# A gated three-branch decoder layer on one core: first loads issued in order of use, a third load buffer, and gate tiles between attention and branch projection

## The chip, the cores and the metric

The kernel runs on one core of a Trainium2 chip. The metric is device time in microseconds (us) of one execution. The core has TensorE (PE in the profile; PEld is its loading of weights), VectorE (DVE), ScalarE (ACT), GpSimd (POOL) and SyncE (SP). In this kernel SP issues every DMA, one after the other.

## What is computed

One decoder layer on 256 tokens of width 2048, in float32:

```python
proj = x @ w_in
q_a, k_a, v_a, z_a, u_g, v_g, z_g, q_c, z_c, g_logit = jnp.split(proj, split_at, axis=-1)
y_a = _moba_attention(q_a, k_a, v_a) * jax.nn.silu(z_a)      # 8 heads, causal
y_g = _spatial_gating(u_g, v_g, w_s, b_s, ln_v_g, ln_v_b) * jax.nn.silu(z_g)
mem_k = (mem @ w_mem_k); mem_v = (mem @ w_mem_v)             # 256 memory tokens
y_c = _memory_attention(q_c, mem_k, mem_v) * jax.nn.silu(z_c)  # 4 heads
gates = jax.nn.sigmoid(g_logit)
merged = (gates[:, :, 0] * (y_a @ w_branch_attn)
          + gates[:, :, 1] * (y_g @ w_branch_sgu)
          + gates[:, :, 2] * (y_c @ w_branch_mem))
y = merged @ w_out
x = _layer_norm(DN_ALPHA * x + y, ln_g, ln_b)
```

The spatial gating applies GELU to u and v, a layer norm to v, and a causal 128x128 mixing matrix for each of 8 channel groups.

## The kernel before

**Precision.** Every float32 operand of a large product is taken apart by split() (lines 57 to 60): ScalarE copies it to a rounded `hi` (line 59), VectorE subtracts to get `lo` (line 60), and PE adds up three products, hi x hi, hi x lo and lo x hi. In the profile `hi` and `lo` are the weights of the classic stream, `sh` and `sl` those of the S stream.

**Start.** mem_values() (8 chunks of `w_mv`) and then mem_keys() (8 chunks of `w_mk`) project the memory tokens. Beside mem_keys the list `x_work` (from x_stages()) prepares x: its hi and lo parts (`xhl`), four sums of its quadrants (`F`) and their parts (`xw`), which are stored to DRAM (`xf`) for later. x comes in two loads of 1 MB (`X`), called in mem_values at kp 5 and 6. After mem_keys six blocks of `w_st` are loaded (s_load) and two S steps prepared (s_prep).

**Two streams.** After that a loop at the end of the function runs two generators in steps. classic() makes the gate tiles (gate_tiles: zc, za, ug), the memory attention, the block attention, the spatial gating and the three branch projections (gated_branch). s_stream() makes the eight 1024-wide projections whose results are taken with tokens on partitions (three pairs of branch gates, v_a and v_g), each unit as seven products M1, M5, M6, M3, M7, M4, M2 of quadrants, two steps each, 112 steps in all. In M5, M6 and M4 VectorE subtracts blocks before the split, in M3 after it (line 289). One S step is 12 matmuls of 512 columns; one classic step is half a tile (8 k-slices, each a matmul of 512 and one of 256 columns) or a quarter of a branch's column block (12 matmuls of 512). The loop takes an S step while

```python
done_s * (C_STEPS - LEAD - TAIL) < (done_c - LEAD) * S_STEPS    # 160, 2, 14; 112
```

so that the S stream ends with classic step 146, whatever that step holds. s_prep prepares two S steps ahead; c_half prepares two halves ahead.

**Small work.** Evacuations go into `late` and are emitted behind the next step's matmuls. Attention heads and the gating's mixing go as lists of stages into `pending`; each tick() emits the next stage of each list. A tile's end calls tick(), gated() calls it too. drain() yields an empty classic step, and further ones with a tick() each until `pending` is empty; classic() runs it before each of the three branch projections, since a branch reads the y of all heads. It takes 4, 4 and 2 steps.

**Loads.** The weights of the classic stream come in chunks of 1 MB, two halves each, in the order of the list `chunks`, into tag `raw` with two buffers. prep_half() splits a half; once both halves of chunk i are split it loads chunk i + 2. Loads and stores of all kinds share SP's queue, and the order of instructions on each engine is made by a planner from the program order, its own estimate of times and the buffers that are free; a load for which a buffer is free can be issued long before its place in the program. `vg` (tag vg, 1 MB) holds the v of the gating, from unit 5 of the S stream to the last mixing.

**End.** merged() transposes the merged branches, 16 chunks of `w_o` give the output projection, and residual() and normalise() finish.

Of the kernel before, what the change touches and what calls it, by code (L numbers as in the profile page):

```python
# [14 lines left out]
P = 128  # L15
# [12 lines left out]
def decoder_layer(ctx, tc, xT, memT, x_tok, w_st, w_mv, w_mk, w_zc, w_qc, w_za, w_qk, w_ug, w_zg,  # L28
# [60 lines left out]

    def load_chunk(i):  # L90
        t = wts.tile([P, 2, 1024], F32, tag="raw", name=f"raw{i}", bufs=2)
        raw[i] = t
        if i < 8:
            a = w2(f"mraw{i}", (P, 2, S))
            act_raw[i] = a
            if i == 0:

                for kk in range(2):
                    nc.sync.dma_start(a[:, kk], memT[:, kk])
                    for c in (slice(0, 512), slice(512, 1024)):  # L100
                        nc.sync.dma_start(t[:, kk, c], chunks[i][:, kk, c])
                return
            nc.sync.dma_start(a, memT[:, 2 * i:2 * i + 2, :])
        for h in range(2) if i < 4 else (slice(0, 2),):
            nc.sync.dma_start(t[:, h], chunks[i][:, h])

    def prep_half():
        i, h = divmod(ptr["half"], 2)
        while ptr["load"] <= min(i + 1, len(chunks) - 1):
            load_chunk(ptr["load"])  # L110
            ptr["load"] += 1
        ptr["half"] += 1
        if i in held_at:
            hi, lo = held_at[i](h)
            split(hi, lo, raw[i][:, h].rearrange("p (k c) -> p k c", c=S))
        else:
            hi = wts.tile([P, 1024], F32R, tag="hi", name=f"hi{i}_{h}", bufs=3)
            lo = wts.tile([P, 1024], F32R, tag="lo", name=f"lo{i}_{h}", bufs=3)
            n = 512 if i == 0 else 1024
            for c in range(0, 1024, n):  # L120
                split(hi[:, c:c + n], lo[:, c:c + n], raw[i][:, h, c:c + n])
            ready.append((hi, lo))
        if h == 1:
            del raw[i]
            if ptr["load"] < len(chunks) and ptr["load"] <= i + 2:
                load_chunk(ptr["load"])
                ptr["load"] += 1
# [6 lines left out]
    for w in (w_mv, w_mk, w_zc, w_qc):  # L134
        chunks += [w[j] for j in range(8)]
    chunks += [w_br[2 * 8 + j] for j in range(8)]
    chunks += [w_za[j] for j in range(8)]
    chunks += [w_qk[j] for j in range(16)]
    chunks += [w_br[j] for j in range(8)]
    chunks += [w_ug[j] for j in range(8)]  # L140
# [13 lines left out]

    for j in range(16):
        if j >= 12:
            pass
# [225 lines left out]
    def mem_values():  # L383
        ps = [[new_acc(f"mv{t}{n}") if t + n < 2 else new_sps(f"mv{t}{n}") for n in range(2)] for t in range(2)]
        for kp in range(8):
            if kp == 0:
                load_chunk(0)
                ptr["load"] = 1
# [6 lines left out]
            for kk in range(2):  # L395
# [9 lines left out]
                if kp in (5, 6) and kk == 0:  # L405
                    x_loads[kp - 5]()
# [30 lines left out]

    for _ in run(mem_values()):
        pass
    for i, _ in enumerate(run(mem_keys())):  # L440
        if i >= 1 and x_work:
            x_work.pop(0)()
    while x_work:
        x_work.pop(0)()
        step(lambda: None)
    for blk in (B11, B12, B22):
        for h in range(2):
            s_load(0, blk, h)
# [12 lines left out]
    def gate_tiles(w, func, d):  # L461

        for j in range(8):
# [209 lines left out]
    def gated_branch(b, order):  # L673
        for n in range(4):
# [6 lines left out]
            for half in range(4):  # L681
# [9 lines left out]
                if half == 3:  # L691
                    late.append(lambda n=n, ps=ps, g=g: gated(b, order, n, ps, g))
                yield
# [39 lines left out]
    def classic():  # L733
# [3 lines left out]
        yield from drain()  # L737
        yield from gated_branch(2, 0)
        yield from gate_tiles("za", AF.Silu, sza_d)
        new_y(0)  # L740
        yield from block_attention()
        yield from drain()
        yield from gated_branch(0, 1)
        yield from gate_tiles("ug", AF.Gelu_apprx_tanh, gu_d)
        new_y(1)
        yield from gating()
        yield from drain()
        yield from gated_branch(1, 2)

    def drain():  # L750

        yield None
        while pending:
            tick()
            yield None
# [142 lines left out]
```

## Time and profile before

| | |
|---|---|
| median of 3 runs | 1037.3 us (1035.51 to 1040.58) |
| profiled execution | 1036.3 us |
| its span, first to last instruction | 1034.6 us |
| mean granted clock of PE | 0.982 |
| busy PE / VectorE / ScalarE | 95% / 80% / 56% of the span |
| DMA | 269.28 MB, mean 260 GB/s |

A busy PE in the profile is not a PE at its peak, since matmuls are pipelined and their ends are modelled; what counts here is where PE has gaps, and where its granted clock is below 1.00. Times in the rows are microseconds from the span's start. A row of a stretch gives for each engine its busy time and the number of its instructions.

### The profile page before, as it was taken

The page shows a single profiled execution, that of the slowest core. Times are in us where ns is not written, and L with a number is a line of the kernel's source. Part 1 is how long each engine was busy: PE and PEld are TensorE (multiplying, and loading weights), DVE is VectorE, ACT ScalarE, POOL GpSimd, SP SyncE. Part 2 cuts the span into 40 slices and gives each one's busy share as a digit, 9 for nine tenths or more (in the row PEclk, how much of TensorE's full clock was granted, in tenths as well). Part 3 has the DMA queues.
Part 4 walks back from the last instruction along what each step waited for, and adds up shares of the span by engine and source line. Part 5 has one row for each costly group of instructions (what it writes and reads, how often), then busy time and mean ns, then how long its engine had stood idle before and what let it go on. Part 6 is the DMA issues. An engine that isn't in the chain of part 4 may idle for free.

```text
span 1034.6 us, 12910 instructions
## 1 busy us (share of the span) xinstructions
PE 987.9 (95%) x4888; PEld 827.9 (80%) x4888; DVE 823.0 (80%) x800; ACT 580.4 (56%) x638; POOL 7.8 (1%) x17
## 2 busy tenths in 40 slices
PE   8699999999998999999999999879989999999995
PEld 6578888888876788888888887658878888888885
DVE  6644897797788889777977998989898685775657
ACT  6433665656556565565655557766546465754440
POOL 0000000000000000000000000000000001000000
PEclk9899999999999999999999999979999999999998
DMA  9997468847945985797389558639958955678642
GB/s 339 416 403 236 170 207 327 359 146 276 337 178 197 371 340 185 264 346 300 132 300 366 175 165 322 238 122 366 413 174 315 309 174 195 222 268 294 225 158 81
DMA packets 68125, 269.28 MB, mean 260 GB/s; under 512 B 7520, under 2 KB 21600, under 8 KB 45536
## 3 DMA queue, kind: packets, MB, share of 16 engines
q1 hardware_dynamic: 68064, 268.47, 70.9%
q8 instruction: 38, 0.62, 0.2%
q14 instruction: 23, 0.19, 0.1%
HBM read 245.37 MB, written 23.07 MB: 259 GB/s over the span
## 4 chain that ended last, share of the span: by engine, by line
PE 74%; DMA 11%; DVE 8%; ACT 3%; issue 3%; SPq 0%; DVEq 0%; ACTq 0%
PE sM L365 7%; PE sM L364 7%; PE sM L366 7%; DMA raw<-in_w_mv_dram 4%; DVE sl L60 3%; PE mk L165 3%; PE q L165 3%; PE za L165 3%; PE zc L165 3%; PE qc L165 3%; PE k L165 3%; PE zg L165 3%; PE o L782 3%; PE o L781 3%; PE o L780 3%
## 5 line engine op out<-in xcount | busy, mean ns | idle before, releaser
L59 ACT ACTIVATE hi<-raw 128x1024 fp32r<-128x1024 f32 (+1 forms) x218 | 227.8, 1050 | 213.4 <-DMA raw<-in_w_o_dram 22.2
L60 DVE TENSOR_TENSOR lo<-raw,hi 128x1024 fp32r<-128x1024 f32 (+1 forms) x218 | 261.8, 1210 | 98.7 <-ACT hi L59 97.7
L60 DVE TENSOR_TENSOR sl<-b,sh 128x2048 fp32r<-128x2048 f32 x112 | 255.9, 2287 | 56.5 <-ACT sh L59 55.8
L59 ACT ACTIVATE sh<-b 128x2048 fp32r<-128x2048 f32 x112 | 214.5, 1915 | 123.2 <-PE sM L365 101.8
L289 DVE TENSOR_TENSOR b<-b,b 128x2048 f32<-128x2048 f32 x64 | 145.8, 2283 | 6.2 <-DMA b<-in_w_st_dram 6.0
L365 PE MATMUL sM<-sl,xf 128*128 128x512 f32 x256 | 103.6, 405 | 5.7 <-DVE sl L60 5.7
L364 PE MATMUL sM<-sh,xf 128*128 128x512 f32 x256 | 102.8, 402 | 1.1 <-ACT sh L59 1.1
L366 PE MATMUL sM<-sh,xf 128*128 128x512 f32 x256 | 102.6, 401 | 0.0
L365 PE MATMUL sM<-sl,xhl 128*128 128x512 f32 x192 | 75.7, 394 | 2.4 <-DVE sl L60 2.4
L364 PE MATMUL sM<-sh,xhl 128*128 128x512 f32 x192 | 76.0, 396 | 0.0
L689 PE MATMUL b<-lo,yhl 128*128 128x512 f32 x192 | 75.0, 391 | 0.5 <-DVE lo L60 0.5
L366 PE MATMUL sM<-sh,xhl 128*128 128x512 f32 x192 | 75.1, 391 | 0.0
L690 PE MATMUL b<-hi,yhl 128*128 128x512 f32 x192 | 74.0, 391 | 1.0 <-DVE yhl L60 1.0
L688 PE MATMUL b<-hi,yhl 128*128 128x512 f32 x192 | 71.7, 391 | 1.6 <-ACT hi L59 1.6
L365 PEld LDWEIGHTS sM<-sl,xf 128*128 128x128 f32 x256 | 49.5, 193 | 17.6 <-DVE sl L60 7.9
L364 PEld LDWEIGHTS sM<-sh,xf 128*128 128x128 f32 x256 | 49.3, 193 | 12.5 <-ACT sh L59 1.7
L366 PEld LDWEIGHTS sM<-sh,xf 128*128 128x128 f32 x256 | 49.5, 193 | 10.6
L165 PE MATMUL ug<-xhl,hi 128*128 128x512 f32 x128 | 45.7, 398 | 3.2 <-ACT hi L59 3.2
L402 PE MATMUL mv<-hi,memhl 128*128 128x512 f32 x128 | 37.9, 407 | 11.1 <-ACT hi L59 11.0
L165 PE MATMUL mk<-memhl,hi 128*128 128x512 f32 x128 | 46.2, 405 | 1.4 <-ACT hi L59 1.4
L165 PE MATMUL q<-xhl,hi 128*128 128x512 f32 x128 | 46.7, 401 | 0.0
L165 PE MATMUL qc<-xhl,hi 128*128 128x512 f32 x128 | 46.2, 400 | 0.0
(296 smaller groups left out, 1845.2 us busy)
## 6 DMA issues: line engine op xcount, KB each, us to landing
b<-in_w_st_dram SPq DMA_DIRECT2D x64, 1024.0 KB, 7.7
xf<-xf SPq DMA_DIRECT2D x64, 512.0 KB, 5.6
raw<-in_w_br_dram SPq DMA_DIRECT2D x24, 1024.0 KB, 6.9
raw<-in_w_qk_dram SPq DMA_DIRECT2D x16, 1024.0 KB, 7.2
raw<-in_w_o_dram SPq DMA_DIRECT2D x16, 1024.0 KB, 4.8
raw<-in_w_mk_dram SPq DMA_DIRECT2D x8, 1024.0 KB, 5.3
raw<-in_w_zc_dram SPq DMA_DIRECT2D x8, 1024.0 KB, 4.9
raw<-in_w_qc_dram SPq DMA_DIRECT2D x8, 1024.0 KB, 7.8
```

Source lines behind the costliest of these rows:

```text
L59: nc.scalar.activation(hi, v, AF.Copy)
L60: nc.vector.tensor_tensor(lo, v, hi.bitcast(F32), op=ALU.subtract)
L165: nc.tensor.matmul(ps, hi, x, start=first, stop=False)
L289: sub = lambda o, x, y: nc.vector.tensor_tensor(o, x, y, op=ALU.subtract)
L364: nc.tensor.matmul(ps, ah, hi[:, c], start=first, stop=False, skip_group_check=True)
L365: nc.tensor.matmul(ps, ah, lo[:, c], start=False, stop=False, skip_group_check=True)
L366: nc.tensor.matmul(ps, al, hi[:, c], start=False, stop=last, skip_group_check=True)
L402: nc.tensor.matmul(ps[t][n], lhs, rhs[:, n * 512:(n + 1) * 512], start=(k == 0 and rhs is hi and lhs is xh[t]), stop=(k == KT - 1 and lhs ...
L688: nc.tensor.matmul(ps[t], yh, hi[:, c], start=(k == 0), stop=False)
L689: nc.tensor.matmul(ps[t], yh, lo[:, c], start=False, stop=False)
L690: nc.tensor.matmul(ps[t], yl, hi[:, c], start=False, stop=(k == 7))
L780: nc.tensor.matmul(ps[:, 0:n], mh, hi, start=first, stop=False)
```

## The change

It does the following.

- Each of the chunks 1 to 15 is issued on SP behind the chunk before it (`issue_after` orders instructions of one queue, it does not wait for data). The two loads of X are issued behind chunks 5 and 6. The six `w_st` blocks are asked for within mem_keys, at its steps 2, 4, 10 and 12, each behind the newest chunk load; `x_work` begins one step earlier.
- Every third of the chunks 0 to 15, and every third of the 16 chunks of `w_o`, goes into the buffer of `vg`; there a load runs up to three chunks ahead instead of two. Between chunk 16 and `w_o` there are two buffers as before.
- drain() goes. Three of the eight za tiles run between memory attention and its branch projection, three of the eight ug tiles between block attention and its projection; the other five follow the projection. The list of chunks follows. Before the third projection, behind the gating, nothing takes drain's place. In the first column block of each projection the steps 0 to 2 call tick().

```diff
@@ -87,8 +87,25 @@
     ptr = {"load": 0, "half": 0}
     hold = {}
 
+    loaded = {}
+    riders = {}
+
     def load_chunk(i):
-        t = wts.tile([P, 2, 1024], F32, tag="raw", name=f"raw{i}", bufs=2)
+
+        if 0 < i < 16:
+            with tc.issue_after(loaded[i - 1].ins):
+                load_one(i)
+        else:
+            load_one(i)
+        for fn in riders.pop(i, ()):
+            with tc.issue_after(loaded[i].ins):
+                fn()
+
+    def load_one(i):
+        if i % 3 == 2 and i < 16 or i >= OUT and (i - OUT) % 3 == 2:
+            t = big.tile([P, 2, 1024], F32, tag="vg", name=f"raw{i}")
+        else:
+            t = wts.tile([P, 2, 1024], F32, tag="raw", name=f"raw{i}", bufs=2)
         raw[i] = t
         if i < 8:
             a = w2(f"mraw{i}", (P, 2, S))
@@ -98,17 +115,23 @@
                 for kk in range(2):
                     nc.sync.dma_start(a[:, kk], memT[:, kk])
                     for c in (slice(0, 512), slice(512, 1024)):
-                        nc.sync.dma_start(t[:, kk, c], chunks[i][:, kk, c])
+                        loaded[i] = nc.sync.dma_start(t[:, kk, c], chunks[i][:, kk, c])
                 return
             nc.sync.dma_start(a, memT[:, 2 * i:2 * i + 2, :])
         for h in range(2) if i < 4 else (slice(0, 2),):
-            nc.sync.dma_start(t[:, h], chunks[i][:, h])
+            loaded[i] = nc.sync.dma_start(t[:, h], chunks[i][:, h])
+
+    def room_after(i):
+
+        return i - 3 if i <= 16 or i >= OUT + 2 else i - 2
+
+    def load_after(c):
+        while ptr["load"] < len(chunks) and room_after(ptr["load"]) <= c:
+            ptr["load"] += 1
+            load_chunk(ptr["load"] - 1)
 
     def prep_half():
         i, h = divmod(ptr["half"], 2)
-        while ptr["load"] <= min(i + 1, len(chunks) - 1):
-            load_chunk(ptr["load"])
-            ptr["load"] += 1
         ptr["half"] += 1
         if i in held_at:
             hi, lo = held_at[i](h)
@@ -122,9 +145,7 @@
             ready.append((hi, lo))
         if h == 1:
             del raw[i]
-            if ptr["load"] < len(chunks) and ptr["load"] <= i + 2:
-                load_chunk(ptr["load"])
-                ptr["load"] += 1
+            load_after(i)
 
     def c_half(ahead=2):
         while len(ready) < ahead + 1 and ptr["half"] < 2 * len(chunks):
@@ -133,11 +154,13 @@
 
     for w in (w_mv, w_mk, w_zc, w_qc):
         chunks += [w[j] for j in range(8)]
+    chunks += [w_za[j] for j in range(3)]
     chunks += [w_br[2 * 8 + j] for j in range(8)]
-    chunks += [w_za[j] for j in range(8)]
+    chunks += [w_za[j] for j in range(3, 8)]
     chunks += [w_qk[j] for j in range(16)]
+    chunks += [w_ug[j] for j in range(3)]
     chunks += [w_br[j] for j in range(8)]
-    chunks += [w_ug[j] for j in range(8)]
+    chunks += [w_ug[j] for j in range(3, 8)]
     chunks += [w_zg[j] for j in range(8)]
     chunks += [w_br[8 + j] for j in range(8)]
 
@@ -152,9 +175,8 @@
             return t[:, :, 0:S], t[:, :, S:2 * S]
         return dst
 
+    OUT = len(chunks)
     for j in range(16):
-        if j >= 12:
-            pass
         chunks.append(w_o[j])
         if j in (4, 7, 10, 13):
             held_at[len(chunks) - 1] = held(*divmod((4, 7, 10, 13).index(j), 2))
@@ -384,8 +406,7 @@
         ps = [[new_acc(f"mv{t}{n}") if t + n < 2 else new_sps(f"mv{t}{n}") for n in range(2)] for t in range(2)]
         for kp in range(8):
             if kp == 0:
-                load_chunk(0)
-                ptr["load"] = 1
+                load_after(-1)
             a = act_raw.pop(kp)
             n = 1 if kp == 0 else 2
             for c in range(0, 2, n):
@@ -402,8 +423,6 @@
                             nc.tensor.matmul(ps[t][n], lhs, rhs[:, n * 512:(n + 1) * 512],
                                              start=(k == 0 and rhs is hi and lhs is xh[t]),
                                              stop=(k == KT - 1 and lhs is xl[t]))
-                if kp in (5, 6) and kk == 0:
-                    x_loads[kp - 5]()
                 yield
 
         def evacuate():
@@ -435,17 +454,22 @@
             step(go)
             yield
 
+    riders[5], riders[6] = [x_loads[0]], [x_loads[1]]
     for _ in run(mem_values()):
         pass
     for i, _ in enumerate(run(mem_keys())):
-        if i >= 1 and x_work:
+        if x_work:
             x_work.pop(0)()
+        if i in (2, 4):
+            with tc.issue_after(loaded[ptr["load"] - 1].ins):
+                s_load(0, B12, i // 2 - 1)
+        if i in (10, 12):
+            for blk in (B11, B22):
+                with tc.issue_after(loaded[ptr["load"] - 1].ins):
+                    s_load(0, blk, i // 2 - 5)
     while x_work:
         x_work.pop(0)()
         step(lambda: None)
-    for blk in (B11, B12, B22):
-        for h in range(2):
-            s_load(0, blk, h)
     s_prep(0)
     s_prep(1)
 
@@ -458,9 +482,9 @@
     def put_y(b, j, y):
         split(yhl[b][:, j, 0:S], yhl[b][:, j, S:2 * S], y)
 
-    def gate_tiles(w, func, d):
-
-        for j in range(8):
+    def gate_tiles(w, func, d, tiles=range(8)):
+
+        for j in tiles:
             def fin(ps, j=j):
                 v = w1(f"{w}{j}")
                 joined(v, ps, f"{w}{j}")
@@ -690,6 +714,8 @@
                         nc.tensor.matmul(ps[t], yl, hi[:, c], start=False, stop=(k == 7))
                 if half == 3:
                     late.append(lambda n=n, ps=ps, g=g: gated(b, order, n, ps, g))
+                elif n == 0:
+                    late.append(tick)
                 yield
 
     def gated(b, order, n, ps, g):
@@ -734,25 +760,17 @@
         yield from gate_tiles("zc", AF.Silu, szc_d)
         new_y(2)
         yield from mem_attention()
-        yield from drain()
+        yield from gate_tiles("za", AF.Silu, sza_d, range(3))
         yield from gated_branch(2, 0)
-        yield from gate_tiles("za", AF.Silu, sza_d)
+        yield from gate_tiles("za", AF.Silu, sza_d, range(3, 8))
         new_y(0)
         yield from block_attention()
-        yield from drain()
+        yield from gate_tiles("ug", AF.Gelu_apprx_tanh, gu_d, range(3))
         yield from gated_branch(0, 1)
-        yield from gate_tiles("ug", AF.Gelu_apprx_tanh, gu_d)
+        yield from gate_tiles("ug", AF.Gelu_apprx_tanh, gu_d, range(3, 8))
         new_y(1)
         yield from gating()
-        yield from drain()
         yield from gated_branch(1, 2)
-
-    def drain():
-
-        yield None
-        while pending:
-            tick()
-            yield None
 
     C_STEPS, S_STEPS = 160, 14 * UNITS
     LEAD, TAIL = 2, 14
```

## Rows read from the trace of the kernel before

**Rows 1.** The page's busy time, share of the span and instructions by engine

```profile
PE 987.9 (95%) x4888; PEld 827.9 (80%) x4888; DVE 823.0 (80%) x800; ACT 580.4 (56%) x638; POOL 7.8 (1%) x17
```

**Rows 2.** Stretches: length; busy PE, PEld, DVE, ACT, POOL; clock; DMA share; GB/s

```profile
20.00:80.00 60.00, 47.64 (x204) 37.46 (x204) 36.32 (x41) 26.74 (x32) 0.00 (x0) 0.91 0.99 402
110.00:862.00 752.00, 731.20 (x3585) 611.58 (x3584) 644.85 (x560) 447.87 (x478) 3.62 (x4) 0.99 0.71 260
```

**Rows 3.** The same view: the three stalled windows in the middle

```profile
300.00:350.00 50.00, 43.48 (x186) 33.58 (x185) 44.64 (x36) 30.30 (x34) 0.00 (x0) 1.00 0.54 193
640.00:700.00 60.00, 48.93 (x193) 37.92 (x192) 53.84 (x59) 41.83 (x48) 0.00 (x0) 0.89 0.55 206
760.00:780.00 20.00, 16.79 (x80) 13.89 (x79) 19.57 (x21) 9.75 (x10) 0.00 (x0) 0.91 0.61 189
```

**Rows 4.** The same view: three stretches without a PE gap

```profile
580.00:610.00 30.00, 30.00 (x160) 25.54 (x159) 30.00 (x27) 16.80 (x22) 0.00 (x0) 1.00 0.41 138
700.00:750.00 50.00, 50.00 (x222) 41.30 (x221) 46.58 (x38) 29.70 (x24) 0.00 (x0) 1.00 1.01 392
900.00:1020.00 120.00, 120.00 (x624) 102.73 (x623) 78.41 (x102) 51.02 (x56) 0.00 (x0) 1.00 0.61 215
```

**Rows 5.** PE's instructions in time: start, length, what, [idle before <-releaser]

```profile
6.36 0.97 PE L402 MATMUL mv<-hi,memhl 128*128 128x512 f32 x3 [0.89 <-ACT hi L59]
...
31.89 2.07 PE L402 MATMUL mv<-hi,memhl 128*128 128x512 f32 x4 [8.01 <-ACT hi L59]
```

**Rows 6.** The SP queue in time, 0 to 35 us: start, length, line, issues

```profile
12.60 1.29 SPq L230 DMA_DIRECT2D X<-in_xT_dram  x2
13.94 1.06 SPq L273 DMA_DIRECT2D b<-in_w_st_dram  x2
15.34 5.28 SPq L105 DMA_DIRECT2D raw<-in_w_mv_dram  x3
```

**Rows 7.** PE's instructions of tile sM (the S stream) by stretch

```profile
630.00:700.00 70.00, 44.28 (x161) 0.90 0.57 213
```

**Rows 8.** PE's instructions of tile b (the branch projections) by stretch

```profile
630.00:700.00 70.00, 12.27 (x48) 0.90 0.57 213
```

**Rows 9.** The chain of 60 to 76 us in time: start, length, what

```profile
64.28 0.28 PE mk L165
64.56 0.12 PE mk L166
64.68 0.23 PE mk L165
```

**Rows 10.** VectorE by line and shape, 110 to 862 us: xcount | busy, mean ns

```profile
L60 DVE TENSOR_TENSOR sl<-b,sh 128x2048 fp32r<-128x2048 f32 x112 | 255.9, 2287 | 56.5 <-ACT sh L59 55.8
L60 DVE TENSOR_TENSOR lo<-raw,hi 128x1024 fp32r<-128x1024 f32 x138 | 166.7, 1218 | 27.5 <-ACT hi L59 27.0 <-PE q L166 0.3
L289 DVE TENSOR_TENSOR b<-b,b 128x2048 f32<-128x2048 f32 x64 | 145.8, 2283 | 6.2 <-DMA b<-in_w_st_dram 6.0
L324 DVE TENSOR_TENSOR k<-sM,k 128x512 f32<-128x512 f32 x31 | 21.2, 684 | 1.9 <-PE sM L366 1.8
L700 DVE TENSOR_TENSOR sg<-b,sg 128x512 f32<-128x512 f32 x16 | 10.6, 682 | 0.0
L639 DVE TENSOR_TENSOR vg<-vg,sc 128x256 f32<-128x256 f32 x16 | 6.2, 420 | 1.8 <-DMA sc<-in_sgu_bc_dram 1.8
...
L612 DVE BATCH_NORM_STATS2 vst<-vg 128x6 f32<-128x512 f32 x4 | 2.7, 686 | 1.8 <-ACT vg L611 1.8
...
L619 DVE TENSOR_SCALAR vg<-vg,vmv,vgr 128x1024 f32<-128x1024 f32 x2 | 1.5, 806 | 0.0
```

**Rows 11.** DMA traffic of the first 100 us

```profile
DMA packets 9640, 34.83 MB, mean 348 GB/s; under 512 B 1040, under 2 KB 2832, under 8 KB 7440
```

**Rows 12.** The waits of all engines: who for whom, us, times, longest

```profile
ACT xw L59 <- DMA xf<-xw: 3.9, 5, 2.0
```

**Rows 13.** ScalarE by line: count, busy us, mean ns

```profile
L467 ACT ACT_TABLE_LOAD x3 | 3.8, 1283 | 0.1
```

## The prediction

> **What bounds the kernel now.** TensorE. I read the page's head first: PE is busy 987.9 of 1034.6 us, VectorE 823.0 [rows 1]. A busy share does not say where the time could go, so the next view is the busy time by stretch, read for two things: where PE idles, and where its granted clock is under 1.00. From 20 to 80 us PE is busy 47.64 of 60 and the clock is 0.91 [rows 2]: 12.4 us idle, and at most 60 x 0.09 = 5.4 us of columns lost at the lower level (1.2 instead of 2.4 GHz for a part of the stretch). From 110 to 862 us PE is busy 731.20 of 752 [rows 2], and all of its 20.8 us of idleness lies in three windows: 6.5 us in 300 to 350, 11.1 in 640 to 700, 3.2 in 760 to 780; the clock there is 1.00, 0.89 and 0.91 [rows 3], at most another 6.6 + 1.8 = 8.4 us. From 900 to 1020 us PE never idles [rows 4]. So what a reordering can win is about 17.8 us at the start and 29.2 us in the middle. The rest of the span is matmuls back to back, the first microseconds, and a tail that the change leaves alone.
>
> Why the start stalls: the waits of PE there are for `hi`, the longest 8.01 us [rows 5], with the clock under 1.00 [rows 2], and `hi` waits for its chunk. The SP queue shows the reason: at 12.60 us it issues both 1 MB loads of X, at 13.94 us two blocks of `w_st`, and only at 15.34 us the next chunk halves of `w_mv` [rows 6]. DMA is at 0.99 of its capacity, 402 GB/s [rows 2], so bytes that nobody needs yet stand ahead of bytes that PE waits for.
>
> Why the middle stalls: two of the windows begin where classic() drains. In 630 to 700 us PE ran 161 matmuls of the S stream (13 steps) and 48 of the branch (4 steps) [rows 7, 8], while the planned ratio is 112 to 144, 0.78 S steps for each classic one. An S step costs PE 12 x 0.23 = 2.8 us [rows 9], and VectorE (255.9 + 145.8 + 21.2) / 112 = 3.8 us [rows 10]. A classic step is 8 x (0.23 + 0.12) = 2.8 us of PE [rows 9] and one `lo`, 1.22 us of VectorE [rows 10]. At 0.78 to 1 VectorE has 4.2 us of work for 5.0 of PE; a run of S steps alone is VectorE's.
>
> **The change part by part.**
>
> *Order of the first loads.* Chunks 1 to 15 are each issued behind the one before, X behind chunks 5 and 6, the six `w_st` blocks behind the newest chunk in steps 2, 4, 10 and 12 of mem_keys. On SP these eight 1 MB loads move behind the `w_mv` chunks; nothing moves on POOL. The bytes stay: the first 100 us move 34.83 MB [rows 11], which is 87 us at the 402 GB/s of [rows 2], while PE needs about 6 us to its first steady matmuls [rows 5], 192 x 0.23 = 44 us for mem_values and 16 x 2.8 = 45 us for mem_keys, 95 us in all. A `w_mv` chunk with its memory tokens is 1.31 MB, 3.2 us, against 5.5 us of PE. So loads in order of use stay ahead.
>
> *The third buffer* holds every third chunk up to 15, and of `w_o`, in the space of `vg`. Of the start it is a part: with two buffers a load has two half steps (5.5 us) to land, with three it has four (11 us), so X's 2.5 us per load fits in between. At the end it buys nothing, since PE is gapless there [rows 4]. If `vg` came free late, chunk OUT+2 would wait; the work that hides it is the two chunks before, 11 us of PE.
>
> *What is late next at the start.* X is issued behind six chunks of 3.2 us, at about 22 instead of 12.6 us, so its splits, sums and eight stores (xhl, F, xw) move from PE's stall into mem_values' end and mem_keys. ScalarE and VectorE run in order, so an `xw` that waits for its store holds `hi` up. The trace has such waits: 3.9 us in 5 times [rows 12]. I leave all 3.9 us as a new cost; the bounds are 0, and the whole 17.8 us if the moved work fills what was freed. The `w_st` blocks can wait at SP's head too, B11 for F and B22 for X, with the chunks of `zc` queued behind them; what hides it is the two chunks already in, 11 us of PE, and without that cover it is inside the upper bound. Start: 17.8 - 3.9 = **13.9 us**.
>
> *The drains go.* Ten empty classic steps (4 + 4 + 2) leave a sequence of 170. Up to the S stream's end at step 146 this makes 146 classic steps instead of 138 for the 112 S steps, and 14 instead of 22 behind it. VectorE's whole work between 110 and 862 us is 644.85 us [rows 2]; it fits into a stretch 29 us shorter at 89%.
>
> *Three gate tiles go between.* Each moves two classic steps, a 1 MB chunk load, a gate store, two `hi`/`lo` pairs and a join ahead of the branch, and on SP ahead of eight `w_br` and the `gl` loads. Their three ticks are the last head's scores, transposes and values, so the y that half 3 of the first column block needs is begun some 4 steps ahead. Cost of the tiles: nothing, they were run later. The switch of activation functions adds some four table loads of 1.28 us on ScalarE [rows 13], hidden by ScalarE's own idleness (41.83 us busy of 60 in its fullest stalled window [rows 3]), 5 us at most without it. In the last branch no tile goes between: the final mix is emitted by the tick behind half 0 and read in half 3, with 2 to 3 steps (6 to 8 us) ahead of seven VectorE operations of 0.42 us [rows 10].
>
> *What VectorE still owes.* Of a unit's seven products M5, M6 and M3 take a subtraction and a split, 4.57 us for 2.8 of PE. Three of these runs of six steps fall on busy classic work. Unit 2 on branch 2: 27.4 + 8 x 1.22 + 4 x 0.68 + 4 x 0.42 = 41.6 us of VectorE against 14 x 2.76 = 38.6 of PE. Unit 6 on branch 0, with gated()'s multiply and an add of the same size, and sgu_norm: 27.4 + 9.8 + 8 x 0.68 + 2 results + 4 x 0.69 + 2 x 0.81 = 48.4 against 38.6. Unit 7 on gating (seven 0.42 us operations for each tile): 27.4 + 9.8 + 11.8 = 49.0 against 39. Owed: 3.0, 9.8 and 10.0 us. Cover is what was prepared ahead, two S steps and two halves, at most 2 x 4.57 + 2 x 1.22 = 11.6 us. The nearest row: in 580 to 610 us VectorE is busy 30.00 of 30 over such a run beside attention, and PE has no gap [rows 4]. I take half of the cover, 5.8 us: 0, 4.0 and 4.2 us remain, 8.2. Bounds: 0 with full cover, 22.8 with none. Middle: 29.2 - 8.2 = **21.0 us**, between 6.4 and 29.2.
>
> The sum stands against the profiled execution, 1036.3 us, 1.7 of it outside the span and 1.0 below the median of the runs: 1036.3 - 13.9 - 21.0 = 1001.4, so **1001 us**; 989 with every bound at its best.
>
> **The rivals.**
>
> *VectorE keeps the middle* (0.20). The change takes nothing from VectorE; if its work can't move to other stretches, the three windows shrink only by its own idleness, 5.36 + 6.16 + 0.43 = 12.0 us [rows 3]: 1036.3 - 13.9 - 12.0 = 1010 us. For it: VectorE is full there. Against it: over the whole stretch it is busy 644.85 of 752 us [rows 2], so there is room outside the windows, and PE was gapless at full VectorE in 580 to 610. The Trainium skill reads it in this way: "Perfetto Trace Analysis", section "Identifying the Most-Contended Engine", takes VectorE's occupancy as a fair measure of how near it is to its limit and wants the engine with the highest occupancy mended first. By that page the order of the tiles would bring little in these windows; the trace agrees for the windows (44.64 of 50, 53.84 of 60 [rows 3]) and not for the whole stretch, where VectorE is under PE [rows 2].
>
> *The start pays back* (0.12). X's work and the `w_st` blocks, packed into mem_keys, delay `hi`, `lo` or the first S step by as much as the loads gained: 1036.3 - 21.0 = 1015 us. For it: DMA was full at the start [rows 2], and three buffers serve eight stores. Against it: 95 us of PE against 87 of DMA.
>
> *The change doesn't do what it says* (0.08). The order on each engine comes from a planner; it may again run S steps ahead where the last head is late, since only the loads are pinned: 1036.3 - 13.9 = 1022 us.
>
> *Slower: chunks come late throughout the branches* (0.10). Between the drains two raw buffers stay, and a load is issued only when VectorE has read the chunk two before it. At 760 us that chain cost PE 3.2 us and some clock, 5.0 us in all [rows 3]. Without pauses it could recur in each of the 16 chunks of branches 2 and 0. It decides from nine of them on (43.1 us of gains / 5.0); at twelve it gives 1036.3 - 43.1 + 60 = 1053 us. Against it: 700 to 750 us, in the middle of a branch, has DMA at 1.01 of capacity and no gap in PE [rows 4].
>
> **How the numbers follow.** The forecast holds 0.50, from 989 to 1008 us. The first two rivals end at 1010 and 1015, so the range is 989 to 1018 us and holds 0.82. A measurement of this kernel can tell 0.5%, 5 us, from no change. Faster: 0.50 + 0.20 + 0.12 + 0.08 = 0.90; of the last rival 0.04 ends near nine late chunks, the same, and 0.06 slower.
>
> **What would show it.** Start: X issued on SP behind chunk 5, no PE wait of 8 us, clock 1.00 through 20 to 80, mem_keys beginning near 52 us instead of 64 [rows 9]. Middle: S and classic matmuls alternate near 0.78 in the windows behind attention, no window with PE under 9 of 10 us, VectorE near full at units 6 and 7 with waits for `sl` if the cover is short. Wrong at the start if waits for `xw` or X stand ahead of `hi`; wrong in the middle if PE idles as much at the branches or, new, in gating.

## The result, and the profile after

The changed kernel takes 1012.68 us (median of 4 runs, 1012.21 to 1014.38) against 1038.94 us before; the ratio is 0.975, interval 0.971 to 0.979. The forecast was 1001 us. The measured time lies inside the range of 989 to 1018 us, which took in two rivals, and outside the 989 to 1008 us of the forecast itself. Of the 34.9 us that the sum promised against the profiled execution, 21.9 came between the two profiled executions (1014.4 us after, spans 1034.6 and 1012.7) and 26.3 between the medians.

PE's work is the same, so the gain must be gaps and clock. The page's first view of the changed kernel, as in [rows 1]:

```profile
PE 982.4 (97%) x4888; PEld 826.9 (82%) x4888; DVE 820.6 (81%) x800; ACT 590.6 (58%) x646; POOL 12.0 (1%) x17
```

Stretches of the changed kernel, columns as in [rows 2]:

```profile
20.00:80.00 60.00, 58.51 (x294) 49.20 (x294) 43.20 (x51) 34.11 (x44) 0.00 (x0) 1.00 0.93 357
100.00:120.00 20.00, 16.71 (x75) 13.30 (x74) 18.36 (x12) 12.74 (x11) 0.00 (x0) 0.91 0.60 203
110.00:862.00 752.00, 740.04 (x3663) 621.34 (x3662) 647.46 (x578) 469.23 (x506) 10.49 (x8) 0.99 0.73 265
300.00:350.00 50.00, 50.00 (x224) 41.51 (x223) 42.43 (x32) 34.28 (x35) 0.00 (x0) 1.00 0.64 218
640.00:700.00 60.00, 54.80 (x222) 43.48 (x221) 53.34 (x52) 44.94 (x48) 0.00 (x0) 0.91 0.62 233
680.00:690.00 10.00, 10.00 (x32) 8.00 (x33) 10.00 (x9) 4.22 (x5) 0.00 (x0) 0.72 0.23 70
740.00:760.00 20.00, 18.47 (x91) 15.25 (x90) 16.49 (x13) 13.72 (x12) 0.00 (x0) 1.00 0.88 341
760.00:790.00 30.00, 25.70 (x134) 21.10 (x134) 30.00 (x29) 15.41 (x18) 3.45 (x1) 1.00 0.47 160
```

Against [rows 2, 3]: the start has 1.5 us of idleness instead of 12.4, and full clock. The first of the three middle windows is closed. The second, at branch 0, is half closed. The third, a late chunk, is gone. Two windows are new: 100 to 120 us, where the S stream begins, and 760 to 790 us, in the gating.

To add gaps and clock up without counting twice, I took for every matmul the time from its start to the next one's start, less the spacing that its shape has back to back (0.228 us for 512 columns, 0.116 for 256, and likewise for the small ones). The spacings add up to 960.7 us in each kernel here, so what is over is comparable (another choice for the small shapes shifts the columns, in all rows much alike). I call it lost time, us by stretch of the one profiled execution:

| kernel | 0 to 100 | 100 to 130 | 280 to 400, branch 2 | 620 to 710, branch 0 | 740 to 800 | rest | sum |
|---|---|---|---|---|---|---|---|
| before | 20.4 | 0.4 | 8.6 | 18.4 | 5.6 | 7.9 | 61.2 |
| after | 5.5 | 5.5 | 0.9 | 11.1 | 7.8 | 8.6 | 39.3 |
| loads only | 5.4 | 5.7 | 8.9 | 18.1 | 7.1 | 7.5 | 52.6 |
| tiles only | 19.4 | 1.1 | 0.1 | 10.2 | 7.6 | 7.6 | 46.0 |
| to chunk 17 | 5.0 | 3.7 | 0.1 | 10.0 | 7.5 | 7.7 | 34.0 |
| six ug tiles | 5.0 | 5.4 | 0.1 | 1.1 | 1.4 | 9.5 | 22.5 |
| no subtractions, unit 5 | 5.2 | 5.4 | 0.3 | 1.5 | 0.8 | 7.7 | 21.0 |
| no subtractions, unit 6 | 4.7 | 5.2 | 0.5 | 1.9 | 1.0 | 7.1 | 20.5 |
| no subtractions, unit 7 | 4.5 | 6.6 | 0.1 | 8.9 | 2.7 | 7.2 | 30.0 |
| to chunk 17 and six ug | 5.2 | 3.5 | 0.1 | 1.1 | 0.9 | 8.6 | 19.4 |
| no pinned order | 16.6 | 0.6 | 0.2 | 9.7 | 7.8 | 7.3 | 42.2 |
| two buffers at the start | 15.0 | 4.9 | 0.9 | 9.3 | 8.5 | 8.8 | 47.3 |
| five ug tiles | 4.9 | 5.3 | 1.5 | 5.9 | 6.4 | 8.1 | 32.0 |
| to chunk 17 and eight ug | 6.2 | 3.4 | 0.4 | 0.8 | 8.3 | 6.6 | 25.7 |

Kernels that run the same code in a stretch differ there by 1 to 2 us (branch 0 with three tiles: 8.9 to 11.1), and differences of that size say nothing. Before to after the sums differ by 21.9 us, which is the difference of the spans. The start gives 14.9 us and the branches and the ug tiles 15.0 (7.7 + 7.3); 5.1 us are lost again at the beginning of the S stream, 2.2 in 740 to 800 us, and 0.7 elsewhere. The 2.2 us are a difference of two things: the late chunk of before is gone, and the gating has new waits.

### The profile page after: what moved, and what is told of

Same layout as the page of the kernel before. It is cut to its first block, busy times and chain, and to the rows that moved or that the text cites. A ratio compares the mean times of both kernels' runs of the same rounds, so it can differ in the third digit from the quotient of the medians.

```text
span 1012.7 us, 12913 instructions
## 1 busy us (share of the span) xinstructions
PE 982.4 (97%) x4888; PEld 826.9 (82%) x4888; DVE 820.6 (81%) x800; ACT 590.6 (58%) x646; POOL 12.0 (1%) x17
## 4 chain that ended last, share of the span: by engine, by line
PE 85%; DVE 5%; ACT 4%; DMA 3%; issue 2%; POOL 0%; SPq 0%; DVEq 0%; ACTq 0%
PE sM L386 9%; PE sM L387 9%; PE sM L388 9%; PE b L713 4%; PE b L714 3%; PE b L712 3%; PE zc L187 3%; PE k L187 3%; PE qc L187 3%; PE za L187 3%; PE q L187 3%; PE mk L187 3%; PE o L800 3%; PE o L799 3%; PE o L798 3%; PE mv L423 3%
## 5 line engine op out<-in xcount | busy, mean ns | idle before, releaser
L386 PE MATMUL sM<-sh,xf 128*128 128x512 f32 x256 | 101.3, 396 | 6.5 <-ACT sh L59 6.5
L387 PE MATMUL sM<-sl,xf 128*128 128x512 f32 x256 | 100.6, 393 | 2.5 <-DVE sl L60 2.5
L388 PE MATMUL sM<-sh,xf 128*128 128x512 f32 x256 | 100.2, 391 | 0.0
L386 PE MATMUL sM<-sh,xhl 128*128 128x512 f32 x192 | 77.4, 403 | 0.0
L388 PE MATMUL sM<-sh,xhl 128*128 128x512 f32 x192 | 76.3, 397 | 0.0
L714 PE MATMUL b<-hi,yhl 128*128 128x512 f32 x192 | 74.9, 394 | 0.0
L712 PE MATMUL b<-hi,yhl 128*128 128x512 f32 x192 | 74.0, 398 | 0.9 <-ACT hi L59 0.9
L386 PEld LDWEIGHTS sM<-sh,xf 128*128 128x128 f32 x256 | 48.3, 189 | 18.3 <-ACT sh L59 7.9
L388 PEld LDWEIGHTS sM<-sh,xf 128*128 128x128 f32 x256 | 48.1, 188 | 10.3
L187 PE MATMUL zc<-xhl,hi 128*128 128x512 f32 x128 | 45.7, 398 | 0.4 <-ACT hi L59 0.4
L187 PE MATMUL k<-xhl,hi 128*128 128x512 f32 x128 | 46.0, 397 | 0.0
## 6 DMA issues: line engine op xcount, KB each, us to landing
raw<-in_w_mk_dram SPq DMA_DIRECT2D x8, 1024.0 KB, 10.1
```

Source lines behind the costliest of these rows:

```text
L187: nc.tensor.matmul(ps, hi, x, start=first, stop=False)
L386: nc.tensor.matmul(ps, ah, hi[:, c], start=first, stop=False, skip_group_check=True)
L387: nc.tensor.matmul(ps, ah, lo[:, c], start=False, stop=False, skip_group_check=True)
L388: nc.tensor.matmul(ps, al, hi[:, c], start=False, stop=last, skip_group_check=True)
L712: nc.tensor.matmul(ps[t], yh, hi[:, c], start=(k == 0), stop=False)
L714: nc.tensor.matmul(ps[t], yl, hi[:, c], start=False, stop=(k == 7))
```

## Experiments

### The two parts apart

Loads only: the changed kernel with the chunks' list, the gate tiles and the drains of before.

```diff
-        yield from gate_tiles("za", AF.Silu, sza_d, range(3))
+        yield from drain()
         yield from gated_branch(2, 0)
...
-                elif n == 0:
-                    late.append(tick)
```

> Only the loads' part of the change: order of the first loads, third buffer; the drains, the list of chunks and the tiles as before. If the parts add up as the two traces say (start 20.3 us lost before against 5.4 after, and 5.2 us newly lost at 100 to 116 us), it gives 1036 - 15 + 5 = 1027 us, with the new stall at 100 to 116 us and the three stalled windows of the middle shifted but whole. Rival: the new stall belongs to the tiles' part; then 1021 us and no stall near 105 us.

Measured: 1026.42 us, ratio 0.990 (0.988 to 0.992), 10.1 us less than before.

Tiles only: the kernel before with the new list of chunks, gate_tiles(..., tiles), no drains and the ticks.

> Only the tiles' part: no drains, three gate tiles between attention and branch, list of chunks and ticks as in the changed kernel; loads as before with two buffers. Sum of the traces: 1036 - 12 = 1024 us, start as before (8 us wait at 24 to 32 us). Rival: the middle depends on the head start of the loads; then under 4 us gained, 1032 us or more.

Measured: 1021.74 us, ratio 0.986 (0.984 to 0.988), 14.8 us less. The parts add up (24.9 us, against 23.9 us from 1036.55, the kernel before measured beside these runs, to 1012.7), so they act in different places and neither needs the other. The loss at 100 to 130 us is the loads' (5.7 alone). The one in the gating is the tiles': with the tiles only, PE waits 0.66 and 1.83 us for `sl` at 775 and 780 us, while the 7.1 us of the loads only are the late chunk before `ug`, a wait of 3.21 us at 758 us and the lower clock behind it.

### The start: order and buffer

No pinned order: everything else as changed.

```diff
-            with tc.issue_after(loaded[i - 1].ins):
+            if True:
...
-                with tc.issue_after(loaded[ptr["load"] - 1].ins):
+                if True:
```

> The changed kernel without the pinned order (no issue_after anywhere): the third buffer and everything else stay. If the order is what the start gains by, X and w_st stand ahead of chunk 4 again, PE waits some 7 us for hi near 24 to 32 us, and the loss of the first 95 us is near 17 us instead of 5: about 1020 us, less what the stall at 100 to 116 us gives back (up to 5). Rival: the third buffer alone is enough, 1012 to 1014 us.

Measured: 1018.59 us, ratio 0.983 (0.980 to 0.986). The SP queue in time, and PE's instructions behind it with their idleness:

```profile
13.05 0.65 SPq L252 DMA_DIRECT2D X<-in_xT_dram  x1
...
15.63 0.55 SPq L252 DMA_DIRECT2D X<-in_xT_dram  x1
...
16.98 1.61 SPq L295 DMA_DIRECT2D b<-in_w_st_dram  x2
19.59 4.22 SPq L122 DMA_DIRECT2D raw<-in_w_mv_dram  x3
```

```profile
35.92 2.07 PE L423 MATMUL mv<-hi,memhl 128*128 128x512 f32 x4 [6.66 <-ACT hi L59]
```

X and `w_st` stand ahead of the chunks again, as in [rows 6], and the wait of [rows 5] is back with 6.66 us: one chunk more in hand puts it off by 4 us and does not remove it. The changed kernel's queue at the same place:

```profile
15.36 0.33 SPq L122 DMA_DIRECT2D raw<-in_w_mv_dram  x1
...
18.74 0.33 SPq L122 DMA_DIRECT2D raw<-in_w_mv_dram  x1
19.11 0.65 SPq L252 DMA_DIRECT2D X<-in_xT_dram  x1
```

Two buffers: order as changed, the third buffer only for `w_o`.

```diff
-        if i % 3 == 2 and i < 16 or i >= OUT and (i - OUT) % 3 == 2:
+        if i >= OUT and (i - OUT) % 3 == 2:
...
-        return i - 3 if i <= 16 or i >= OUT + 2 else i - 2
+        return i - 3 if i >= OUT + 2 else i - 2
```

> The changed kernel with the pinned order but only two buffers for chunks 0 to 15 (the third stays for w_o). By the prediction X's 2.5 us per load fit only with the third buffer: with two a chunk has 5.5 us to land behind X, so waits for hi of 2 to 4 us at about two places, 1015 to 1020 us. Rival: order alone suffices at the start, since 3.2 us of DMA for each chunk stand against 5.5 of PE: 1012 to 1014 us.

Measured: 1020.78 us, ratio 0.984 (0.981 to 0.987). The waits of PE from 20 to 100 us (who for whom, us, times, longest):

```profile
PE mv L423 <- DVE lo L60: 2.9, 3, 1.2
PE mk L187 <- ACT hi L59: 2.3, 3, 1.4
PE mk L188 <- DVE lo L60: 2.3, 3, 0.8
```

The time is just over the 1015 to 1020 us expected (the four runs go from 1016.5 to 1022.4 us, and the profiled one is the slowest). The place was not the one I expected: no long wait behind X, but nine short ones over mem_values and mem_keys, with the clock at 0.91 in 80 to 100 us. The first 100 us lose 15.0 us. So of the 15 us that the start gained, neither the order nor the buffer gives much alone: order without buffer 5 (20.4 to 15.0), buffer without order 4 (to 16.6), both 15. The buffer gives a chunk time to land beside other transfers; the order keeps 4 MB of those from coming before it.

### The new loss at 100 to 120 us

The pinned order and the third buffer carried on to chunks 16 and 17:

```diff
-        if 0 < i < 16:
+        if 0 < i < 18:
...
-        if i % 3 == 2 and i < 16 or i >= OUT and (i - OUT) % 3 == 2:
+        if i % 3 == 2 and i < 18 or i >= OUT and (i - OUT) % 3 == 2:
...
-        return i - 3 if i <= 16 or i >= OUT + 2 else i - 2
+        return i - 3 if i <= 19 or i >= OUT + 2 else i - 2
```

> The changed kernel with the third buffer and the pinned order carried on to chunks 16 and 17, so that chunk 17 (second tile of zc) needs chunk 14's end instead of chunk 15's and is issued ahead of the last w_st blocks. If the stall at 100 to 116 us is chunk 17 landing late behind 4 MB of w_st, it goes: 1012.7 - 5 = 1007 to 1008 us. Rival: it is the third S step's preparation, which has to wait for the end of mem_keys in any case; then the stall stays and the time is 1012 to 1013.

The changed kernel's SP queue shows chunk 17 (the second load of `zc`) issued 13 us after chunk 16, because its buffer comes free with chunk 15, and with the last four `w_st` blocks ahead of it; it landed 9.1 us after its issue:

```profile
85.57 0.33 SPq L122 DMA_DIRECT2D raw<-in_w_zc_dram  x1
86.76 2.86 SPq L295 DMA_DIRECT2D b<-in_w_st_dram  x2
...
90.15 0.90 SPq L295 DMA_DIRECT2D b<-in_w_st_dram  x2
...
98.89 0.38 SPq L122 DMA_DIRECT2D raw<-in_w_zc_dram  x1
```

Behind the first zc tile PE has three S steps in a row, and it waited for the third one's `sh` (PE's instructions with their idleness):

```profile
109.28 0.80 PE L386 MATMUL sM<-sh,xf 128*128 128x512 f32 x1 [2.84 <-ACT sh L59]
...
117.12 0.50 PE L187 MATMUL zc<-xhl,hi 128*128 128x512 f32 x1 [0.45 <-ACT hi L59]
```

That `sh` was late on ScalarE. Its queue first idled for 5.16 us until the zc tile had ended, and then had another `sh`, a load of a function table and the tile's SiLU ahead of it:

```profile
103.51 0.39 ACT L207 ACTIVATE zc0l<-zc 128x256 f32<-128x256 f32 x1 [5.16 <-PE zc L188]
103.79 1.91 ACT L59 ACTIVATE sh<-b 128x2048 fp32r<-128x2048 f32 x1
105.72 1.28 ACT L491 ACT_TABLE_LOAD   x1
107.02 0.42 ACT L491 ACTIVATE zc<-zc 128x256 f32<-128x256 f32 x1
107.34 1.89 ACT L59 ACTIVATE sh<-b 128x2048 fp32r<-128x2048 f32 x1
```

Measured with the order carried on: 1007.98 us, ratio 0.973 (0.970 to 0.975), 4.7 us under the changed kernel by the medians (2.4 by the ratios; the four runs of each don't overlap). Chunk 17 goes at 90.96 us and the 2.84 us wait is gone, but the loss in the stretch falls only from 5.5 to 3.7 us; the rest of the gain lies elsewhere, in columns that differ by no more than their scatter. So the late chunk is shown for a part of the stall, about 1.8 us. Short waits for `hi` and `lo` of zc stay, 2.4 us together, and ScalarE idles there too, 5.26 us until the zc tile's end.

### Branch 0: the last head or unit 6

The forecast had put what remains at branch 0 down to unit 6's subtractions, sgu_norm and gated(). The trace offered another cause. PE's and VectorE's rows of the changed kernel:

```profile
645.54 0.60 PE L575 MATMUL s<-kT,qT 128*128 128x256 f32 x2
...
661.77 0.59 PE L604 MATMUL o<-ptT,vah 128*128 128x256 f32 x2
```

```profile
674.42 0.41 DVE L60 TENSOR_TENSOR yhl<-sza,yhl 128x256 fp32r<-128x256 f32 x1
```

Those are the last head's scores, values and y. The last quarter of a branch's column block (half 3) can't be finished without that y. Its k tile ended at 598 us and the first ug tile, whose tick emits the scores, at 607; the scores ran at 645. PE's matmuls of the S stream and of the branch, 640 to 680 us, one row each:

```profile
640.00:680.00 40.00, 26.68 (x97) 0.94 0.64 243
```

```profile
640.00:680.00 40.00, 8.47 (x34) 0.94 0.64 243
```

8 S steps and 3 of the branch: the run of S steps that [rows 7, 8] showed for the drain, without a drain. PE's waits in it:

```profile
667.71 0.50 PE L386 MATMUL sM<-sh,xf 128*128 128x512 f32 x1 [2.38 <-ACT sh L59]
...
677.38 0.49 PE L712 MATMUL b<-hi,yhl 128*128 128x512 f32 x1 [0.91 <-ACT hi L59]
679.19 0.79 PE L386 MATMUL sM<-sh,xf 128*128 128x512 f32 x1 [1.31 <-ACT sh L59]
```

They are for ScalarE's results, and both engines behind them are full: ScalarE is busy 9.91 and 9.85 of 10 us from 650 to 670, VectorE all 30 us of 660 to 690. Three experiments separate the causes. Six ug tiles ahead of the branch, with the list of chunks in the same order, everything still computed:

```diff
-        yield from gate_tiles("ug", AF.Gelu_apprx_tanh, gu_d, range(3))
+        yield from gate_tiles("ug", AF.Gelu_apprx_tanh, gu_d, range(6))
         yield from gated_branch(0, 1)
-        yield from gate_tiles("ug", AF.Gelu_apprx_tanh, gu_d, range(3, 8))
+        yield from gate_tiles("ug", AF.Gelu_apprx_tanh, gu_d, range(6, 8))
```

> The changed kernel with six instead of three ug tiles ahead of branch 0. If the 11 us lost at 650 to 690 us are the last head's y, late because VectorE's joins and stages of head 7 are behind unit 5's subtractions, 30 us more of other work hide it: at most 3 us lost there, 1004 to 1006 us. Rival: unit 6's subtractions, sgu_norm and gated() fall on the branch whatever comes first; the loss stays near 10 us, 1011 to 1014.

Measured: 997.16 us, ratio 0.962 (0.960 to 0.964), 15.5 us under the changed kernel. The same stretch, columns as above:

```profile
640.00:700.00 60.00, 59.51 (x279) 49.48 (x279) 53.83 (x52) 45.44 (x53) 0.00 (x0) 1.00 0.70 256
```

```profile
670.08 0.42 DVE L60 TENSOR_TENSOR yhl<-sza,yhl 128x256 fp32r<-128x256 f32 x1
```

The last y comes at 670 us, almost when it did; the branch now begins at 661 instead of 630 and finds it in time. VectorE does as much as before the edit (53.83 us against 53.34), and S steps 86 to 91, unit 6's subtracting ones, still fall on branch steps. So unit 6 on the branch alone costs at most the 1.1 us of that column.

Taking subtractions away, in s_prep():

```diff
         sub = lambda o, x, y: nc.vector.tensor_tensor(o, x, y, op=ALU.subtract)
+        if u == 5:
+            sub = lambda o, x, y: None
```

> The changed kernel, with the eight block subtractions of unit 5 (products M5, M6, M3, M4: 18 us of VectorE between about 573 and 640 us) left out, so v of the gating is another. If the last head's chain is late because its joins and stages queue behind these subtractions, head 7's scores come over 10 us earlier than at 645 us, the branch's half 3 is not held until 674 us, and of the 11 us lost at 650 to 690 us at most 3 remain: 1003 to 1006 us. Rival: unit 6, sgu_norm and gated() on the branch make the loss; then 9 us or more stay, 1011 to 1013.

Measured: 996.11 us, one run. The scores ran at 617.09 us and the last y at 636.64 us, 38 us earlier than in the changed kernel:

```profile
617.09 0.60 PE L577 MATMUL s<-kT,qT 128*128 128x256 f32 x2
```

```profile
636.64 0.43 DVE L60 TENSOR_TENSOR yhl<-sza,yhl 128x256 fp32r<-128x256 f32 x1 [1.14 <-ACT yhl L59]
```

With `u == 6` instead:

> The changed kernel with the eight subtractions of unit 6 left out (a gate of branch 1 is another): 18 us of VectorE between about 660 and 720 us. If unit 6 on the branch is the cause, the loss at 650 to 690 us falls from 11 to 2 us or less. If the last head's late y is the cause, head 7's scores stay at 645 us and its y near 670, PE still runs S steps only until then, and lacks less because each needs less of VectorE: 4 to 7 us stay. Both: 1002 to 1008 us, told apart by the place of the scores and the steps in 650 to 675 us.

Measured: 995.56 us, one run. The scores stay late, at 644 us, and the last y comes at 665, yet only 1.9 us are lost in 620 to 710 us, where I had written 4 to 7 for the late y by itself. ScalarE is as full there as in the changed kernel (9.89 and 9.97 of 10 us from 650 to 670), so ScalarE alone is not the cause.

So both are needed for the loss. Unit 5's subtractions delay the last head by some 38 us, and the planner fills the wait at the branch with S steps; those happen to be unit 6's subtracting ones, with which VectorE doesn't keep up. Take either away, or let the branch come later, and the loss goes. How much of the 38 us is the planner's order and how much VectorE's speed these runs don't settle, but speed is not all of it. The delay builds up: against the run without unit 5's subtractions the join of the last k is 18.5 us late, the scores 28.5, the y 37.8. And VectorE, full from 570 to 610 us (39.65 of 40), is busy only 5.39 us of the next 10. It makes that join, whose input ScalarE had left at 599 us, right behind an idleness of 3.63 us in which it waits for the head before:

```profile
618.04 0.42 DVE L608 TENSOR_TENSOR sza<-o,sza 128x256 f32<-128x256 f32 x1 [3.63 <-PE o L605]
618.38 0.41 DVE L208 TENSOR_TENSOR kT<-k,k7l 128x256 f32<-128x256 f32 x1
```

There the order of VectorE's queue held the join, not VectorE's speed.

Five tiles, to see where it turns:

> The changed kernel with five instead of three ug tiles ahead of branch 0. The last y came at 668 to 674 us with three and with six tiles alike; each tile with its share of S steps moves the branch by some 10 us from 630. With five the branch begins near 650 and needs that y near 663: a wait of 5 to 10 us with S steps in it, 2 to 5 us lost, 999 to 1003 us. Rival: a threshold, anything above three is enough: 997 us as with six.

Measured: 1005.80 us, ratio 0.970 (0.967 to 0.973), over the 999 to 1003 expected. At branch 0 5.9 us are lost, more than the 2 to 5 expected, and 6.4 in the last window: between three (11.1) and six (1.1), so not everything above three is enough.

### The gating

The edit of unit 5 with `u == 7`:

> The changed kernel with the eight subtractions of unit 7 left out (the other gate of branch 1 is another): 18 us of VectorE between about 755 and 830 us. If the 5.6 us newly lost at 760 to 790 us, in the gating, are VectorE's debt from unit 7, they fall to 1 us or less: 1007 to 1008. Rival: they come from the mask on GpSimd that the mixing waits for, or from chunk loads; then at least 4 us stay, 1011 to 1013.

Measured: 1005.03 us, one run. In 760 to 790 us PE has no gap, and VectorE is at 20.08 us instead of 30.00:

```profile
760.00:790.00 30.00, 30.00 (x163) 25.74 (x162) 20.08 (x20) 16.04 (x20) 0.29 (x1) 1.00 0.56 196
```

So VectorE's work there sets that loss, the 1.80 us wait of the mixing for GpSimd's mask included, which goes with it. But with six ug tiles the same work stands in the same stretch and costs nothing:

```profile
760.00:790.00 30.00, 30.00 (x162) 25.63 (x161) 30.00 (x27) 18.34 (x21) 8.68 (x2) 1.00 0.55 204
```

There VectorE is as full and PE has no gap. In the kernels with tiles ahead of the branches the loss in the gating goes with the one at branch 0: 6.4 to 8.5 us in 740 to 800 us where branch 0 loses 5.9 or more and unit 7 is whole, 0.8 to 1.4 where branch 0 loses under 2; only the kernel with eight tiles, in which the gating follows the branch at once, breaks this. That is also why six tiles and the runs without the subtractions of units 5 and 6 came out 6 to 7 us under the ranges that I had expected, which counted on branch 0 alone.

How the first loss brings the second is open. At 690 us, counted by PE's matmuls, the S stream of the changed kernel is 6.4 classic steps ahead of its plan, and on plan with six tiles, so that unit 7's subtractions meet the gating's own work elsewhere. But being ahead does not decide it: without unit 6's subtractions it is 6.5 steps ahead and the last window loses 1.0 us, and with five tiles it is 1.1 ahead and 6.4 us are lost.

### Both mends together

> Both at once: buffer and order carried to chunk 17, and six ug tiles ahead of branch 0. The two losses lie 500 us apart; if they are independent the gains add: 1012.7 - 4.7 - 15.5 = 992.5 us. Rival: the planner places the middle otherwise once the start is shorter; then 996 or more.

Measured: 994.84 us, ratio 0.960 (0.958 to 0.962), 42 us under the kernel before, and the fastest that computes everything. The gains nearly add (992.5 expected).

With all eight ug tiles ahead:

> Buffer and order carried to chunk 17, and all eight ug tiles ahead of branch 0, which then stands between the ug tiles and the gating. If the wait for the last y is the whole matter, two more tiles than six add nothing: 994 to 996 us. Rival: branch 0 now runs into unit 7's subtractions and the gating follows without a pause, 3 us or more lost at 690 to 800 us: 998 or more.

Measured: 997.91 us, ratio 0.962 (0.958 to 0.966): not to be told from six by the time alone. The four runs go from 994.18 to 1000.76 us, and the profiled one is the slowest. It shows what the rival named: branch 0 loses 0.8 us, and 8.3 us are lost in 770 to 800 us, where the gating follows the branch without a tile between. PE's instructions there:

```profile
779.29 0.50 PE L387 MATMUL sM<-sl,xf 128*128 128x512 f32 x1 [1.44 <-DVE sl L60]
...
793.55 0.80 PE L187 MATMUL zg<-xhl,hi 128*128 128x512 f32 x1 [3.29 <-ACT hi L59]
```

## Why the prediction was right, and where not

**The start** was forecast at 13.9 us of gain and gave 14.9 up to 100 us, by the mechanism named: X behind chunk 5, PE without a long wait, mem_keys from 53.3 us on (52 forecast). The cost I had left for X's moved work, 3.9 us, was about half of that: the largest wait in its place is 1.49 us for `lo` at 47 us. That order and buffer need each other I had said only of the buffer; the runs show it of both.

**The w_st blocks** were the step that failed at the start. I had written that chunks of zc may queue behind them and that the two chunks already in hide it, 11 us. Only chunk 16 was in; chunk 17's buffer comes free with chunk 15, and behind 4 MB it landed 9.1 us after its issue. I had counted the cover for three buffers in a place where only two are left, and the sum had this term at nothing. The loss there is 5.1 us more than before; with it the start gave 9.8 us net, not 13.9. Carrying the buffer on took back about 1.8 us, and ScalarE's order behind the first zc tile was not in the sum at all.

**Branch 2** was forecast without loss and has 0.9 us. The tiles do there what they were said to: unit 1's subtractions lie well ahead of the last head (the last ends at 251 us, the branch begins at 301).

**Branch 0** was forecast to keep 4.0 us and kept 11.1. The step that failed is "the y that half 3 of the first column block needs is begun some 4 steps ahead". It took the order in which the program emits the stages for the order in which they run. With unit 5's subtractions on VectorE (in the 580 to 610 us of [rows 4], which I had read as harmless because PE had no gap in it), the head's joins and stages came 38 us late. As I read it, PE had no gap because the debt was put on work that nobody waited for yet. The rival that the planner again runs S steps ahead was right in this window, wrong in the other. Two of the signs that I had named for the middle failed with it: PE is busy 7.62 and 7.78 of 10 us from 660 to 680, and 8 S steps ran beside 3 of the branch.

**Unit 6 and unit 7.** The tally of VectorE against PE was no forecast of a loss: unit 6 on the branch was charged 4.0 us and loses at most 1.1 with six tiles; unit 7 was charged 4.2, and the whole last window loses 1.4 with six tiles, while the changed kernel has the new waits in the gating that I had named as a sign of being wrong. Either the cover is larger than the 5.8 us that I took, or the planner spreads VectorE's work further than the tally allows; no run separates the two.

**The table loads** of ScalarE were 8 more and not some four (30 against 22, and 590.6 us of ScalarE against 580.4). I had them hidden by ScalarE's idleness. In general they are, but one stands in ScalarE's chain ahead of the wait at 109 us, and four in the 650 to 670 us in which ScalarE is full.

**The two nearest rivals.** The measured time lies between the rivals at 1010 and 1015 us, and neither is its cause. *VectorE keeps the middle* is refuted in its mechanism: with six tiles PE is busy 59.51 of 60 us at 53.83 us of VectorE. The Trainium skill's page "Perfetto Trace Analysis", section "Optimization Strategy", says that regimes with different bottlenecks may be improved by interleaving them; the six-tile run agrees, with 15.5 us from order alone.

*The start pays back* is right in kind and not in size: the first S steps paid back 5.1 of the 14.9 us. That the total fell inside the range is in part luck: of the 13.0 us missed between the profiled executions 4.1 are the start's, in the manner of this rival, and 7.1 are branch 0's, whose mechanism is nearest to the rival at 1022 us, outside the range.

**Slower**, by late chunks, did not happen. In 740 to 760 us PE still waits 1.53 us for the `hi` of a ug tile, but its chunk, issued at 728.0 us, had landed at 739.2; ScalarE turned to it at 745.69, behind a join's copy, an `sh`, a table load and a GELU.

## What to carry to other kernels

Where a planner or a queue decides the order, ask of each result not when the program emits it but when it ran in the trace, and follow low-priority work through a stretch in which its engine is full: a stretch without a gap on the critical engine can still be building the debt of the next. A pinned order of loads and a spare buffer are worth little apart; carry both on to the point where the next consumer's chunks are in. Fill between a producer and its consumer has an amount that can be found: here three tiles left 11.1 of 18.4 us, five 5.9, six 1.1, and eight moved a loss elsewhere in the profiled run.

## What the runs showed of the hardware

A wait costs more than its length, and the busy time hides it: from 680 to 690 us of the changed kernel PE is busy all 10.00 us, at a granted clock of 0.72, and matmuls of 512 columns stand 0.43 us apart instead of 0.23, as the chain of work shows:

```profile
682.04 0.43 PE b L713
682.47 0.43 PE b L714
```

That is the lower level of the two (1.2 instead of 2.4 GHz). The granted clock is 0.93, 0.84 and 0.72 in the three stretches of 10 us from 660 on. The matmuls stand 0.43 us apart from about 669 to 672 us, right behind the wait of 2.38 us, and from about 680 to 685 us, right behind those of 0.91 and 1.31 us. These are all the waits of PE over 0.2 us in 660 to 690 us.
